# Stores of X held back by the kernel's own clocks, a last norm summed on TensorE, and conditioning blocks used with a margin

## The chip, the cores and the metric

One core of one Trainium2 chip runs the whole program; the seven other cores are idle. The time is device microseconds of one execution. Three runs of the kernel before gave 2848.49, 2847.53 and 2843.91 us, so their median is 2847.53 us. One more execution was recorded by the hardware profiler: 2844.86 us, of which 2843.1 us lie between its first and its last instruction (the span). Every duration below is from that execution.

## The reference

Two layers of a diffusion trunk are computed in float32 for 1152 positions of 1024 features each: 128 positions of a prompt, conditioned by `c_ctx`, and 1024 of a sample, conditioned by `c`.

```
for l in range(2):
    shift1, scale1, gate1, shift2, scale2, gate2 = split(silu(cond) @ w_ada[l] + b_ada[l])   # 1024 x 6144
    h = rmsnorm(x, norm_g[l, 0]) * (1 + scale1) + shift1
    y = attention_and_retention(h) @ w_o        # layer 0
    y = chunk_gmlp(h) @ w_out                   # layer 1
    x = x + gate1 * y
    h = rmsnorm(x, norm_g[l, 1]) * (1 + scale2) + shift2
    x = x + gate2 * ((silu(h @ w_gate) * (h @ w_up)) @ w_down)
y = x * rsqrt(mean(x * x, features) + 1e-6) * final_norm_g
```

The change touches the last line (the final norm), the way in which X is laid off in device memory, and the products with `w_ada` (the conditioning).

## The kernel before, in words

**Layout.** X stands transposed: 8 blocks of 128 features on the partitions, positions along the columns. The positions are cut into two chunks `c` of two pieces `h` with 288 columns each, so a piece of a feature block `f` is a tile of 128x288 (`xp(f, c, h)`), and `xp2` is two blocks side by side. Chunk 0 lies in the tiles x0 and x1, chunk 1 in x2 and x3. A factor of a product is split into a high and a low part (a cast on ACT, a subtraction on DVE or POOL), and each product of TensorE is three: high by high, high by low, low by high. Such a set of 24 products of 288 columns makes one feature block of one piece.

**Weights.** The class `Stream` loads all weights in one fixed order through three staging slots `ST` of 512 KB (issued by SP) and casts them into five ring slots `w`. `pump` takes the next item of the list as soon as a condition on the clocks holds, and in the order of the list alone. An item of kind `w` is a weight unit: its cast stands on ACT, its subtraction on DVE, and then its slot of `ST` is free. An item of kind `pair` is two blocks of `w_ada`: they are multiplied out of `ST` at once, by four products of 32x512 into one PSUM bank (`PS<-ST,S` in the rows), and then two of the three slots are free. Eight pairs make one third of a layer's conditioning.

**What sets the order.** Nothing runs by itself: the Python program writes each engine's instructions down in one order, and each engine works through its own queue in that order. To choose the order the program keeps rough clocks (`Clocks`): `clk.t["T"]` is where it believes TensorE to be, and `clk.ready(tiles)` when it believes that these tiles are written. `tick()` after each group of products calls `pump` and `fill`; `fill` writes down pieces of background work (norms, splits of activations) when the clocks say that their inputs are there. A pair is written down once `clk.ready` of its two blocks is not later than TensorE's clock. A store of X to device memory (`pspill` for two feature blocks of a piece) is written onto SP's queue at once, when its instruction that makes X has been written down; SP waits for that instruction and holds all loads behind it.

**Projection into X** (`proj_out`, once in each layer). 32 sets of 24 products are added to X (`resid`, DVE), squared (ACT) and summed (DVE). When a piece of chunk 0 is complete, `rscale` normalizes it in place (8 DVE and 8 ACT instructions for each piece), and `rsplit` makes seven split operands of it: casts of 128x576 on ACT, differences and subtractions of the same width on DVE. Meanwhile TensorE goes on with chunk 1 and needs a new weight unit for each set of 24 products there.

**The end of the program** (`mixer.run(last1, done1)`). The last group of the second FFN's output product is done for chunk 0 (`down`), then for chunk 1 by `down2`, first for the feature blocks 0, 1, 4, 5 and then for 2, 3, 6, 7. After each step `last1` puts the squares of the finished blocks into the background queue: Square on ACT into one of two buffers, an add on DVE into the running sum `acc2`, and on ACT the multiplication by the gain `final_norm_g`. When all eight blocks of a piece are in the sum, `rstd` sums over the partitions by six products with `ones` of two columns, takes the root (ACT) and the reciprocal (DVE) of 96x12 values, spreads them to a diagonal (DVE), and multiplies that by `ones` to get a 128x288 tile of factors for each piece (copied by ACT). `done1` then multiplies X by the factors, two blocks at a time (128x576, DVE), and stores each on SP's queue to the output.

Of the kernel before, what the change touches and what calls it, by code (L numbers as in the profile page):

```python
# [13 lines left out]
P = 128  # L14
# [118 lines left out]
def body(nc, tc, ap):  # L133
# [88 lines left out]
    class Stream:  # L222
# [11 lines left out]
        def pump(self, force=False):  # L234
            moved = True
            while moved:
                moved = False
                while self.di < min(self.hold, len(self.items)) and self.st:
                    it = self.items[self.di]
                    it["st"] = self.st.popleft()  # L240
                    n = 1
                    for d in it["shape"]:
                        n *= d
                    dst = ST[:, it["st"], :n]
                    if len(it["shape"]) == 2:
                        dst = dst.rearrange("p (a b) -> p a b", a=it["shape"][0])
                    it["v"] = dst
                    it["n"] = n
                    if it["load"] is not None:
                        it["load"](dst)  # L250
                    else:
                        SY.dma_start(out=dst, in_=it["src"])
                    self.di += 1
                    moved = True
                if self.pi < self.di and self.pi not in self.stops:
                    it = self.items[self.pi]
                    now = clk.t["T"] + 1.0
                    if it["kind"] == "block":
                        continue
                    if it["kind"] == "pair":  # L260
                        if self.pi + 1 >= self.di:
                            continue
                        two = self.items[self.pi + 1]
                        if not force and clk.ready([it["v"], two["v"]]) > clk.t["T"]:
                            continue
                        it["fn"](it["v"], two["v"])
                        self.st += [it["st"], two["st"]]
                        self.pi += 1
                    elif it["kind"] == "w":
                        if not self.ring:  # L270
                            continue
                        if not force and clk.ready([it["v"]]) > now:
                            continue
                        r = self.ring.popleft()
                        ring_new(r)
                        g = self.prep(it, r)
                        if att[0] and not force:
                            self.gens[r] = bg_add(g)
                        else:
                            run(g)  # L280
                        self.ready.append(r)
                    else:
                        if len(self.ring) < it["need"]:
                            continue
                        if not force and clk.ready([it["v"]]) > clk.t["T"]:
                            continue
                        it["fn"](it["v"])
                        self.st.append(it["st"])
                    self.pi += 1
                    moved = True  # L290
                    if force and it["kind"] == "w":
                        return
# [84 lines left out]
                moved = True  # L377

    def tick():
        W.pump()  # L380
        fill()

# [95 lines left out]
    def xp2(i, c, h):  # L478
        return xh(c, i // 2)[:, 2 * (i % 2):2 * (i % 2) + 2, h]

    def pspill(i, c, h):
        o = piece(c, h)
        SY.dma_start(out=xtd[:, 2 * i:2 * i + 2, o:o + HN], in_=xp2(i, c, h))

    def preload(c, q, h):
        o = piece(c, h)
# [73 lines left out]

    def xnorm(l, w, c):

        yield from rstd(c)
        A, B = acol[l][w], mod[l][:, 24 * w:24 * w + 8]
        ts = [SC[:, 1728 + HN * i:2016 + HN * i] for i in range(4)]
        for h in range(2):
            r = acc2(c)[:, HN * h:HN * h + HN]
            sg = psegs(c, h)
            dst = [[z[:, f, piece(c, h):piece(c, h) + HN] for f in range(8)] for z in (Hh, Hl)]

            def first(f):
                for cond, s in sg:
                    V.scalar_tensor_tensor(ts[f % 4][:, s], xp(f, c, h)[:, s], A[:, f, cond:cond + 1], r[:, s],
                                           ALU.mult, ALU.mult)

            def split(f):
                t, hi, lo = ts[f % 4], dst[0][f], dst[1][f]
                for cond, s in sg:
                    S.activation(R(hi[:, s]), t[:, s], AF.Identity, bias=B[:, f, cond:cond + 1])
                for cond, s in sg:  # L580
                    V.scalar_tensor_tensor(R(lo[:, s]), t[:, s], B[:, f, cond:cond + 1], hi[:, s], ALU.add, ALU.subtract)
            for f in range(3):
                first(f)
            for f in range(8):
                split(f)
                if f + 3 < 8:
                    first(f + 3)
                if f == 7:
                    hn[0] = 2 * c + h + 1
                yield  # L590
# [24 lines left out]

    def rscale(l, c, h):

        yield from rstd(c, (h,))
        A, B = acol[l][1], mod[l][:, 24:32]
        r = acc2(c)[:, HN * h:HN * h + HN]  # L620
        for f in range(10):
            if f < 8:
                for cond, s in psegs(c, h):
                    x = xp(f, c, h)[:, s]
                    V.scalar_tensor_tensor(x, x, A[:, f, cond:cond + 1], r[:, s], ALU.mult, ALU.mult)
            if f > 1:
                for cond, s in psegs(c, h):
                    x = xp(f - 2, c, h)[:, s]
                    S.activation(x, x, AF.Identity, bias=B[:, f - 2, cond:cond + 1])
            yield  # L630
        scaled.add((c, h))
# [1838 lines left out]
    yield "E"  # L2470


    def last1(c, m):
        for f in (m, m + 4):
            for h in range(2):
                x = xp(f, c, h)
                bg3.append(squares(c, h, f, lambda x=x, f=f: S.activation(x, x, AF.Copy, scale=P2[:, 19 + f:20 + f])))

    def done1(c):
        def gen():  # L2480
            yield from rstd(c)
            for h in range(2):
                r = acc2(c)[:, HN * h:HN * h + HN].unsqueeze(1).to_broadcast([P, 2, HN])
                for i in range(4):
                    x = xp2(i, c, h)
                    V.tensor_tensor(x, x, r, ALU.mult)
                    o = piece(c, h)
                    SY.dma_start(out=ap["o_y"][2 * i:2 * i + 2, :, o:o + HN].rearrange("f p t -> p f t"), in_=x)
                    yield
        g = bg_add(gen())  # L2490
        if c:
            drain(g)

    mixer.run(last1, done1)
    while bg:
# [56 lines left out]
```

## Time and profile before

| what | value |
|---|---|
| runs | 2843.91, 2847.53, 2848.49 us |
| median | 2847.53 us |
| profiled execution | 2844.86 us, span 2843.1 us |
| PE (TensorE) busy | 2689.3 us, 95% of the span |
| DVE, ACT, POOL busy | 63%, 41%, 18% |
| DMA | 457.67 MB, mean 161 GB/s |
| mean granted TensorE clock | 0.983 of full speed |

PE is busy nearly throughout, so time is to be looked for in the stretches in which it stands, and at the two ends. A row of the timeline gives the start, the time to the end of the last of its instructions, the engine, the operation with its output and inputs, their count, and in brackets how long the engine had stood and what it had waited for. All instructions are recorded by one helper and so carry one line number (L129); they are told apart by their tiles. `w` is the ring of weights, `hq` and `h` are split activations, `PS` is PSUM, `SC` scratch.

### The profile page before, as it was taken

Reading aid. Unit: us, or ns where it says so; the run is one execution under the profiler, and the core shown is the slowest. Engines: PE = TensorE matmul, PEld = TensorE weight load, DVE = VectorE, ACT = ScalarE, POOL = GpSimd, SP = SyncE. Lnnn points to the kernel's source line nnn. Section 1 sums busy time; section 2 is a strip of 40 time slices with the busy share of each in tenths; the row PEclk is TensorE's granted clock in tenths of the full one; section 3 lists DMA queues with packets and bytes.
Section 4 is the critical chain, followed back from the end, with each engine's and each line's share of the span. In section 5 each row is a group of like instructions: output and inputs, shape, how many; then the busy total and the mean of one; then the engine's idle time right before and its main releaser. Section 6 shows DMA issues by size and latency. Waiting matters only on the chain.

```text
span 2843.1 us, 49004 instructions
## 1 busy us (share of the span) xinstructions
PE 2689.3 (95%) x18859; PEld 2536.9 (89%) x18859; DVE 1787.7 (63%) x3606; ACT 1167.8 (41%) x2389; POOL 514.5 (18%) x570
## 2 busy tenths in 40 slices
PE   6989998999999999999999899998999999999996
PEld 5987897988988999999899877798999999999995
DVE  5651235888577565665788763456666666558876
ACT  5552224777455333333322351234544344332224
POOL 1120013665100000000465300000000000016551
PEclk9999998999999999999999999999999999999998
DMA  9386426323433444538877442352334343578761
GB/s 301 90 271 207 131 72 188 90 57 96 156 111 120 144 169 140 181 128 273 270 236 251 142 154 82 111 169 77 113 124 162 108 157 124 189 267 267 233 211 67
DMA packets 455328, 457.67 MB, mean 161 GB/s; under 512 B 25963, under 2 KB 399478, under 8 KB 453558
## 3 DMA queue, kind: packets, MB, share of 16 engines
q1 hardware_dynamic: 400272, 360.83, 41.3%
q10 hardware_dynamic: 54822, 93.70, 8.9%
q8 instruction: 149, 2.44, 0.4%
q14 instruction: 85, 0.70, 0.1%
HBM read 312.52 MB, written 141.93 MB: 160 GB/s over the span
## 4 chain that ended last, share of the span: by engine, by line
PE 62%; DVE 9%; ACT 4%; DMA 4%; issue 2%; POOL 1%; ACTq 0%; SPq 0%; DVEq 0%; POOLq 0%
PE PS L129 62%; DVE x L129 4%; DVE SC L129 2%; DVE w L129 2%; DMA hcd<-SC 2%; ACT x L129 1%; ACT w L129 1%; ACT SC L129 1%; DVE hq L129 1%; POOL ST L129 1%; DMA x<-xtd 0%; DMA w<-krd 0%; DMA ST<-in_w_ada 0%; DVE ST L129 0%; ACTq L129 0%
## 5 line engine op out<-in xcount | busy, mean ns | idle before, releaser
L129 PE MATMUL PS<-hq,w 128*128 128x288 f32 (+1 forms) x10644 | 1547.5, 302 | 62.6 <-ACT SC L129 16.2
L129 PEld LDWEIGHTS PS<-hq,w 128*128 128x128 f32 x10644 | 1484.3, 189 | 99.1 <-ACT w L129 20.8
L129 DVE TENSOR_TENSOR w<-ST,w 128x512 fp32r<-128x512 f32 (+3 forms) x539 | 382.1, 725 | 294.8 <-ACT w L129 290.4
L129 ACT CAST w<-ST 128x512 fp32r<-128x512 f32 (+3 forms) x717 | 375.2, 552 | 420.8 <-POOL ST L129 274.3
L129 DVE SCALAR_TENSOR_TENSOR x<-PS,mod,x 128x288 f32<-128x288 f32 (+2 forms) x944 | 389.5, 445 | 124.5 <-PE PS L129 119.4
L129 POOL TENSOR_TENSOR w<-ST,w 128x256 fp32r<-128x256 f32 (+1 forms) x178 | 126.9, 729 | 1592.2 <-ACT w L129 970.2
L129 PE MATMUL PS<-h,w 128*128 128x288 f32 (+1 forms) x2522 | 386.8, 298 | 10.7 <-DVE SC L129 7.3
L129 PEld LDWEIGHTS PS<-h,w 128*128 128x128 f32 (+1 forms) x2522 | 350.6, 188 | 21.5 <-DVE SC L129 9.7
L129 ACT COPY SC<-PS 128x576 f32<-128x576 f32 (+8 forms) x245 | 124.3, 510 | 259.8 <-PE PS L129 218.5
L129 PE MATMUL PS<-x,w 128*128 128x288 f32 (+1 forms) x1440 | 218.8, 299 | 1.8 <-ACT adac L129 1.4
L129 PEld LDWEIGHTS PS<-x,w 128*128 128x128 f32 x1440 | 203.0, 188 | 4.2 <-ACT h L129 1.8
L129 DVE TENSOR_TENSOR SC<-PS,SC 128x576 f32<-128x576 f32 (+3 forms) x146 | 94.1, 646 | 169.0 <-PE PS L129 149.0
L129 POOL TENSOR_TENSOR ST<-ST 128x256 f32<-128x256 f32 (+1 forms) x192 | 139.9, 729 | 150.6 <-DVE w L129 134.6
L129 PEld LDWEIGHTS PS<-w,hq 128*128 128x128 f32 x648 | 120.5, 188 | 38.9 <-issue 11.4
L129 PE MATMUL PS<-w,hq 128*128 128x512 f32 x648 | 154.6, 396 | 0.0
L129 DVE TENSOR_TENSOR SC<-SC 128x288 f32<-128x288 f32 (+5 forms) x215 | 104.4, 494 | 57.5 <-ACT SC L129 41.4
L129 ACT ACTIVATE SC<-SC 128x576 f32<-128x576 f32 (+2 forms) x89 | 56.9, 639 | 192.2 <-DVE SC L129 180.5
L129 PE MATMUL PS<-w,w 96*128 96x512 f32 x384 | 109.2, 420 | 4.7 <-ACT w L129 2.7
L129 DVE TENSOR_TENSOR SC<-SC,x 128x576 fp32r<-128x576 f32 (+1 forms) x90 | 68.0, 756 | 69.6 <-DMA hcd<-SC 50.7
L129 DVE TENSOR_REDUCE sm<-PS 128x1 f32<-128x1152 f32 (+1 forms) x72 | 89.0, 1236 | 21.9 <-PE PS L129 21.1
L129 ACT ACTIVATE SC<-x 128x288 f32<-128x288 f32 x128 | 55.2, 440 | 114.8 <-DVE x L129 92.4
L129 DVE TENSOR_TENSOR ST<-ST 128x512 f32<-128x512 f32 x144 | 98.8, 686 | 1.8
(191 smaller groups left out, 2475.9 us busy)
## 6 DMA issues: line engine op xcount, KB each, us to landing
hq<-hcd SPq DMA_DIRECT2D x106, 576.0 KB, 9.1
hcd<-x ACTq DMA_DIRECT2D x180, 288.0 KB, 2.2
ST<-in_w_ada SPq DMA_DIRECT2D x80, 512.0 KB, 4.2
h<-hcd SPq DMA_DIRECT2D x48, 576.0 KB, 7.3
ST<-in_w_ffn_gate SPq DMA_DIRECT2D x52, 512.0 KB, 4.0
ST<-in_w_ffn_up SPq DMA_DIRECT2D x52, 512.0 KB, 3.9
hcd<-SC ACTq DMA_DIRECT2D x72, 288.0 KB, 3.3
ST<-in_w_ffn_down SPq DMA_DIRECT2D x80, 256.0 KB, 5.4
```

Of the source, the lines that this page charges most:

```text
L129: return fn(*args, **kw)
```

## The change

1. In `pump`, a pair of conditioning blocks is written down only when TensorE's clock is 1.5 us past the time at which the blocks are believed to have landed (before: 0).
2. `pspill` puts a store of X into a list `due`; `spill_due`, called at each `tick`, writes it onto SP's queue once TensorE's clock is 3.0 us past the time at which X is believed to be made. `xnorm` and `rscale` first write down all stores of their piece that are still in the list.
3. At the end, chunk 0's second piece is scaled and stored after all products instead of between them. For chunk 1 the first four feature blocks go through the old running sum; the squares of the last four go each into a buffer of its own and are summed over features and partitions at once on PE, by float32 products of 128x288 with the 128x128 `ones` into two PSUM banks (ten products: eight squares and the two running sums). The root is taken on 128x288 values (ACT), the reciprocal too (DVE), and there are no diagonal, spreading products and copies any more. The multiplications by the gain stand in two groups of four after the squares, and chunk 1's eight stores alternate between ACT's and SP's queues.

```diff
@@ -261,7 +261,7 @@
                         if self.pi + 1 >= self.di:
                             continue
                         two = self.items[self.pi + 1]
-                        if not force and clk.ready([it["v"], two["v"]]) > clk.t["T"]:
+                        if not force and clk.ready([it["v"], two["v"]]) + 1.5 > clk.t["T"]:
                             continue
                         it["fn"](it["v"], two["v"])
                         self.st += [it["st"], two["st"]]
@@ -377,6 +377,7 @@
                 moved = True
 
     def tick():
+        spill_due()
         W.pump()
         fill()
 
@@ -478,9 +479,19 @@
     def xp2(i, c, h):
         return xh(c, i // 2)[:, 2 * (i % 2):2 * (i % 2) + 2, h]
 
+
+    due = deque()
+
     def pspill(i, c, h):
         o = piece(c, h)
-        SY.dma_start(out=xtd[:, 2 * i:2 * i + 2, o:o + HN], in_=xp2(i, c, h))
+        due.append((c, h, xtd[:, 2 * i:2 * i + 2, o:o + HN], xp2(i, c, h)))
+
+    def spill_due(which=None):
+
+        for z in list(due):
+            if z[:2] == which or which is None and clk.ready([z[3]]) + 3.0 < clk.t["T"]:
+                SY.dma_start(out=z[2], in_=z[3])
+                due.remove(z)
 
     def preload(c, q, h):
         o = piece(c, h)
@@ -560,6 +571,8 @@
 
     def xnorm(l, w, c):
 
+        for h in range(2):
+            spill_due((c, h))
         yield from rstd(c)
         A, B = acol[l][w], mod[l][:, 24 * w:24 * w + 8]
         ts = [SC[:, 1728 + HN * i:2016 + HN * i] for i in range(4)]
@@ -615,6 +628,7 @@
 
     def rscale(l, c, h):
 
+        spill_due((c, h))
         yield from rstd(c, (h,))
         A, B = acol[l][1], mod[l][:, 24:32]
         r = acc2(c)[:, HN * h:HN * h + HN]
@@ -2470,26 +2484,65 @@
     yield "E"
 
 
+    def gcol(c, h, f):
+        x = xp(f, c, h)
+        S.activation(x, x, AF.Copy, scale=P2[:, 19 + f:20 + f])
+
     def last1(c, m):
+        if c and m > 1:
+            return
         for f in (m, m + 4):
             for h in range(2):
-                x = xp(f, c, h)
-                bg3.append(squares(c, h, f, lambda x=x, f=f: S.activation(x, x, AF.Copy, scale=P2[:, 19 + f:20 + f])))
+                bg3.append(squares(c, h, f, lambda h=h, f=f: gcol(c, h, f)))
+
+    def scaled_out(c, h, r):
+        for i in range(4):
+            x = xp2(i, c, h)
+            V.tensor_tensor(x, x, r.unsqueeze(1).to_broadcast([P, 2, HN]), ALU.mult)
+            o = piece(c, h)
+            (SY if i % 2 or not c else S).dma_start(out=ap["o_y"][2 * i:2 * i + 2, :, o:o + HN].rearrange("f p t -> p f t"), in_=x)
+            yield
 
     def done1(c):
         def gen():
-            yield from rstd(c)
+            yield from rstd(0)
             for h in range(2):
-                r = acc2(c)[:, HN * h:HN * h + HN].unsqueeze(1).to_broadcast([P, 2, HN])
-                for i in range(4):
-                    x = xp2(i, c, h)
-                    V.tensor_tensor(x, x, r, ALU.mult)
-                    o = piece(c, h)
-                    SY.dma_start(out=ap["o_y"][2 * i:2 * i + 2, :, o:o + HN].rearrange("f p t -> p f t"), in_=x)
-                    yield
-        g = bg_add(gen())
-        if c:
-            drain(g)
+                if h:
+                    yield lambda: False
+                yield from scaled_out(0, h, acc2(0)[:, HN * h:HN * h + HN])
+        if c == 0:
+            bg_add(gen())
+            return
+        while bg3:
+            bg_step(bg3)
+
+
+        a = acc2(1)
+        sums = [PS[:, 4 + h, :HN] for h in range(2)]
+        root = [SC[:, 576 + HN * h:][:, :HN] for h in range(2)]
+        late = [(0, 2), (0, 3), (1, 6), (1, 7), (1, 2), (1, 3), (0, 6), (0, 7)]
+
+        def add(h, q, st, sp):
+            TE.matmul(sums[h], lhsT=ones, rhs=q, start=st, stop=sp, skip_group_check=True)
+        for n, (h, f) in enumerate(late):
+            q = SC[:, 1728 + HN * n:][:, :HN] if n < 6 else adac[:, 0:HN] if n == 6 else ST[:, 0, 0:HN]
+            S.activation(q, xp(f, 1, h), AF.Square)
+            add(h, q, n in (0, 2), n in (5, 7))
+            if n == 3:
+                for z in range(2):
+                    add(z, a[:, HN * z:HN * z + HN], False, False)
+        for f in (2, 3, 6, 7):
+            gcol(1, 1, f)
+        for h in (1, 0):
+            S.activation(root[h], sums[h], AF.Sqrt, bias=epsc, scale=1.0 / 1024.0)
+        for f in (2, 3, 6, 7):
+            gcol(1, 0, f)
+        while bg:
+            bg_step()
+        for h in (1, 0):
+            V.reciprocal(root[h], root[h])
+            for _ in scaled_out(1, h, root[h]):
+                pass
 
     mixer.run(last1, done1)
     while bg:
```

**Order on PE, where the second head group's keys are projected, just ahead of the retention's values (layer 0).** `ST,S` are the conditioning products of a pair, `hq,w` three chunks' products with one weight unit, `w,hq` the values' products; of the twelve equal rows `hq,w` ahead of it, the last five stand. Before:

```order
L129 MATMUL PS<-hq_20_535,w_32_1715 128x384 x6
L129 MATMUL PS<-ST,S_92 32x512 x4
L129 MATMUL PS<-hq_13_219,w_32_1715 128x384 x6
L129 MATMUL PS<-hq_17_331,w_32_1715 128x384 x6
L129 MATMUL PS<-hq_19_465,w_32_1715 128x384 x6
L129 MATMUL PS<-hq_20_535,w_32_1715 128x384 x6
L129 MATMUL PS<-ST,S_92 32x512 x4
L129 MATMUL PS<-w_33_1848,hq_13_219 128x512 x6
L129 MATMUL PS<-w_34_1852,hq_17_331 128x512 x6
L129 MATMUL PS<-w_35_1856,hq_19_465 128x512 x6
L129 MATMUL PS<-ST,S_92 32x512 x4
```

The same place now:

```order
L129 MATMUL PS<-hq_13_219,w_32_1715 128x384 x6
L129 MATMUL PS<-hq_17_331,w_32_1715 128x384 x6
L129 MATMUL PS<-hq_19_465,w_32_1715 128x384 x6
L129 MATMUL PS<-hq_20_535,w_32_1715 128x384 x6
L129 MATMUL PS<-ST,S_92 32x512 x4
L129 MATMUL PS<-w_33_1848,hq_13_219 128x512 x6
L129 MATMUL PS<-w_34_1852,hq_17_331 128x512 x6
L129 MATMUL PS<-w_35_1856,hq_19_465 128x512 x6
L129 MATMUL PS<-w_37_1970,hq_20_535 128x512 x6
L129 MATMUL PS<-ST,S_92 32x512 x4
```

The first pair shown has moved behind the four rows `hq,w` (24 products of 384 columns), and from there on four rows of the values' products stand between two pairs instead of three.

**Order on ACT in layer 1's `proj_out`, while chunk 0's second piece is normalized (`x<-x,mod`) and split (`hq<-x`, `h<-x`).** `w_141` to `w_143` are the weight units that PE needs next, one after the other; `SC<-x` are squares. Before:

```order
L129 CAST w_141_17535<-ST 128x1024
L129 ACTIVATE SC<-x_104_11716 128x288
L129 ACTIVATE x_101_11572<-x_101_11572,mod_94 128x288 x4
L129 ACTIVATE x_102_11573<-x_102_11573,mod_94 128x288 x4
L129 CAST hq_13_219<-x_101_11572 128x2x288 x2
L129 CAST hq_17_331<-x_102_11573 128x2x288 x2
L129 CAST h_139_17473<-x_102_11573 128x576 x2
L129 CAST hq_20_535<-x_101_11572 128x2x288 x2
L129 CAST hq_19_465<-x_102_11573 128x2x288 x2
L129 CAST h_138_17472<-x_101_11572 128x576 x2
L129 CAST h_140_17474<-x_102_11573 128x576 x2
L129 CAST w_142_17618<-ST 128x1024
```

The same place now:

```order
L129 CAST hq_13_219<-x_101_11572 128x2x288 x2
L129 CAST hq_17_331<-x_102_11573 128x2x288 x2
L129 CAST w_141_17560<-ST 128x1024
L129 ACTIVATE SC<-x_104_11716 128x288
L129 CAST h_139_17472<-x_102_11573 128x576 x2
L129 CAST hq_20_535<-x_101_11572 128x2x288 x2
L129 CAST w_142_17604<-ST 128x1024
L129 ACTIVATE SC<-x_104_11716 128x288
L129 CAST hq_19_465<-x_102_11573 128x2x288 x2
L129 CAST h_138_17471<-x_101_11572 128x576 x2
L129 CAST h_140_17473<-x_102_11573 128x576 x2
L129 CAST w_143_17649<-ST 128x1024
```

The unit w_141 has moved from ahead of the normalization to behind the first four casts of the split, and w_142 from behind the split into its middle.

**Order on DVE at the end of the program, after the last additions into X.** `x_156`, `x_157` are chunk 0, `x_158`, `x_159` chunk 1; `x<-x,SC` multiplies by the factors. One piece of the difference:

```order
-L129 TENSOR_TENSOR SC<-SC 128x288 x13
-L129 RECIPROCAL rs_100<-rs_100 96x12
-L129 TENSOR_TENSOR SC<-ident,rs_100 96x576
+L129 TENSOR_TENSOR x_156_22498<-x_156_22498,SC 128x2x288 x2
+L129 TENSOR_TENSOR x_157_22499<-x_157_22499,SC 128x2x288 x2
+L129 RECIPROCAL SC<-SC 128x288
 L129 TENSOR_TENSOR x_158_22500<-x_158_22500,SC 128x2x288 x2
 L129 TENSOR_TENSOR x_159_22642<-x_159_22642,SC 128x2x288 x2
+L129 RECIPROCAL SC<-SC 128x288
 L129 TENSOR_TENSOR x_158_22500<-x_158_22500,SC 128x2x288 x2
 L129 TENSOR_TENSOR x_159_22642<-x_159_22642,SC 128x2x288 x2
```

Thirteen adds of the running sums have gone from behind the last addition into X; chunk 0's four multiplications and two reciprocals over 288 columns have come.

## Rows read from the trace of the kernel before

**Rows 1.** The page: span and instructions, busy time of each engine.

```profile
span 2843.1 us, 49004 instructions
PE 2689.3 (95%) x18859; PEld 2536.9 (89%) x18859; DVE 1787.7 (63%) x3606; ACT 1167.8 (41%) x2389; POOL 514.5 (18%) x570
```

**Rows 2.** Waits: engine, for whom, us in total, times, longest.

```profile
PE PS L129 <- DMA ST<-in_w_ada: 7.6, 4, 2.9
PEld PS L129 <- DMA ST<-in_w_ada: 10.4, 8, 3.1
SPq L129 <- DVE x L129: 280.5, 59, 48.9
```

**Rows 3.** Timeline of PE, 229 to 258 us.

```profile
229.77 8.60 PE L129 MATMUL PS<-hq,w 128*128 128x384 f32 x48
241.25 2.87 PE L129 MATMUL PS<-ST,S 128*32 128x512 f32 x8 [2.88 <-DMA ST<-in_w_ada]
244.04 5.37 PE L129 MATMUL PS<-hq,w 128*128 128x384 f32 x24
249.34 1.06 PE L129 MATMUL PS<-ST,S 128*32 128x512 f32 x8
...
254.67 1.05 PE L129 MATMUL PS<-ST,S 128*32 128x512 f32 x4
256.85 1.05 PE L129 MATMUL PS<-ST,S 128*32 128x512 f32 x4 [1.13 <-DMA ST<-in_w_ada]
```

**Rows 4.** Windows: us, PE busy (count), granted clock, DMA share, GB/s.

```profile
244.00:246.00 2.00, 2.00 (x8) 0.50 0.75 225
1985.00:1990.00 5.00, 0.67 (x2) 0.50 0.00 0
2830.00:2834.00 4.00, 2.47 (x6) 0.50 0.01 2
```

**Rows 5.** Timeline of layer 1's proj_out, 1973 to 2001 us.

```profile
1973.32 2.39 ACT L129 CAST hq<-x 128x576 fp32r<-128x576 f32 x4
...
1988.23 1.04 ACT L129 CAST w<-ST 128x1024 fp32r<-128x1024 f32 x1
...
1989.33 0.85 PE L129 MATMUL PS<-hq,w 128*128 128x288 f32 x2 [9.47 <-ACT w L129]
...
1990.73 10.04 PE L129 MATMUL PS<-hq,w 128*128 128x288 f32 x64 [0.56 <-DVE w L129]
```

**Rows 6.** Timeline of PE in layer 0's proj_out, same stage.

```profile
803.49 5.65 PE L129 MATMUL PS<-hq,w 128*128 128x288 f32 x22 [4.08 <-DVE w L129]
...
810.81 8.69 PE L129 MATMUL PS<-hq,w 128*128 128x288 f32 x64 [0.73 <-DVE w L129]
```

**Rows 7.** Timeline of the end of the program, 2816 to 2843 us.

```profile
2816.88 0.96 PE L129 MATMUL PS<-h,hq 128*128 128x288 f32 x6
...
2817.68 0.93 DVE L129 SCALAR_TENSOR_TENSOR x<-PS,mod,x 128x288 f32<-128x288 f32 x2
...
2828.10 2.08 PE L129 MATMUL PS<-ones,SC 128*96 128x2 f32 x12 [10.26 <-DVE SC L129]
...
2833.02 0.40 ACT L129 COPY SC<-PS 128x288 f32<-128x288 f32 x1 [2.54 <-PE PS L129]
2833.45 5.44 DVE L129 TENSOR_TENSOR x<-x,SC 128x576 f32<-128x576 f32 x8 [1.85 <-ACT SC L129]
2833.98 0.40 ACT L129 COPY SC<-PS 128x288 f32<-128x288 f32 x1 [0.56 <-PE PS L129]
```

**Rows 8.** Groups of instructions: busy us, mean ns; squares of the end from 2790.

```profile
L129 ACT ACTIVATE SC<-x 128x288 f32<-128x288 f32 x19 | 8.2, 432 | 13.4 <-DVE SC L129 10.8 <-DVE x L129 2.6
L129 DVE RECIPROCAL sm<-sm 128x1 f32<-128x1 f32 x72 | 10.5, 156 | 11.4 <-ACT SC L129 11.3
L129 DVE RECIPROCAL rcn<-rcn 128x18 f32<-128x18 f32 x4 | 1.1, 266 | 9.0 <-ACT rcn L129 9.0
```

**Rows 9.** The output's stores: us from issue to landing.

```profile
DMA to landing us min/median/max: 2.2/2.3/3.0
```

## The prediction

> **What bounds the kernel now.** I read the page's busy times first: PE works 2689.3 us of the 2843.1 us span, 95% [rows 1]. No other engine comes near, so an edit pays only where it shortens a stretch in which PE stands or runs slowly, or the tail behind PE's last product. Second the waits, for who stands for whom: PE stood 7.6 us in four places for blocks of w_ada, and SP's queue 280.5 us for the instructions that make X [rows 2]. Third the timeline around those places, and the windows for the clock: where PE had just stood, the granted clock was 0.50, the lower level of 1.2 GHz [rows 4], so a stall costs more than its gap. Fourth the timeline of the last 27 us.
>
> The terms are summed against the profiled execution, 2844.86 us (1.76 outside its span). It lies 2.67 below the median of the runs, 2847.53, and inside their spread; I carry the difference over to the median.
>
> **Part 1, the margin: -7.2 us.** The first stalled pair stands behind 48 products that end at 229.77+8.60 = 238.37; the next pair starts at 249.34 [rows 3]. These 10.97 us held one pair (1.06) and 24 products, worth half of 8.60 = 4.30 but taking 5.37 after the stall, at clock 0.50. So 10.97-1.06-4.30 = 5.6 us were lost. Now the 24 products stand ahead of that pair, which PE reaches at 242.67. The blocks had landed by 244.04-1.06 = 242.98 at the latest, as the second four products ran to 244.04. That leaves at most 0.3 us: gain 5.3 to 5.6, I take 5.4. Two pairs on, a pair begun at 254.67 ended only at 257.90: 3.23-1.06 = 2.17 lost, since its second block came late. One more group of the values' products ahead of it adds (254.67-250.40)/3 = 1.42 us, so 1.4 to 2.17: I take 1.8. The other 7.6-2.88-1.13 = 3.6 us of the waits lie in layer 1, at pairs that stand where they stood among PE's products: nothing. Part 1 lies between 0 (the loads slip with the pairs) and -7.8; what a slipping load could cost beyond that is the last rival.
>
> **Part 2, the stores: -3.5 us.** The 280.5 us on SP's queue are no time of PE's. The stores' own move I put at nothing: SP takes a load up sooner, but the load still needs a free staging slot, which the casts give. What counts is what the earlier loads do to the written order in layer 1's proj_out. There PE stood from 1989.33-9.47 = 1979.86 for the cast of a weight unit, which ACT did at 1988.23, behind four casts of the split that began at 1973.32 and more of the same piece; PE ran through from 1990.73 [rows 5]. The 10.87 us held two products worth 0.136 each (8.69/64, [rows 6]), so 10.6 were lost, and the 64 products that follow took 10.04 instead of 8.69: together 11.95.
>
> Now the units w_141 and w_142 stand among the split's casts. Layer 0's proj_out has such an order already and its stall stays: from 803.49-4.08 = 799.41 to 810.81 less 24x0.136 = 3.3 us of products is 8.1 us lost [rows 6]. The difference is 3.8. DVE still makes the split's subtractions and each unit's own, so I take -3.5, between 0 (DVE was the limit all along) and -12 (nothing of the stall is left). No wait is added: before a piece is normalized its stores are written down, so they still read X ahead of its change.
>
> **Part 3, the final norm: -7.1 us.** PE's last ordinary product ends at 2816.88+0.96 = 2817.84, DVE's last addition at 2817.68+0.93 = 2818.61. The eight last multiplications end at 2833.45+5.44 = 2838.89 [rows 7], and the span 4.2 later, with stores that land 2.2 to 3.0 us after their issue [rows 9]. This last stretch I keep. Between lay the running sum's adds, a wait of PE of 10.26 us, and products and copies at clock 0.50.
>
> After: four squares and sums may be done earlier; PE adds the rest behind 2817.84. The two old spreading products were 0.96 apart by ACT's copies (2833.02, 2833.98) [rows 7], at clock 0.50 [rows 4]; at full clock that is 0.48. The first piece's sum is closed by the eighth product: 2817.84+8x0.48 = 2821.7. ACT's last two squares (0.43 each, [rows 8]) follow DVE's addition at 2818.61 and end near 2819.5, ahead of that, as do the four gain multiplications. Root 0.40 and its handing over: 2822.3. No row has a reciprocal of 288 columns. One column takes 156 ns and 18 take 266 [rows 8]: 6.47 ns per column, so 0.156+287x0.00647 = 2.01 us. Four multiplications take 4x0.68 = 2.72. Both pieces one after the other on DVE: 2822.3+2x(2.01+2.72) = 2831.76, or 2838.89-2831.76 = 7.1 earlier. Chunk 0's four moved multiplications, 2.72 us, fit on DVE between 2818.61 and 2821.7, while it waits for the root; without that cover they cost 2.72.
>
> Bounds: a reciprocal as fast as a multiplication of 576 columns (0.68) gives -9.8; one that scales with the 18-column row (266/18x288 = 4.26) gives -2.6. If PE has fallen to clock 0.50 by 2817.84, the eight products last to 2825.5: -3.3. Both ill bounds together: +1.2. I stay with 2.01 us, since two rows give a slope, and with full clock, since PE has just been busy.
>
> The Trainium skill ("VectorE: DVE Perf Modes", section "First, the fixed hardware budget") says that a reciprocal is an iterative divide with a repeat count of 8. If the repeats were eight cycles per column at that page's 0.96 GHz, 288 columns would be an estimated 2.55 us with the 156 ns row as a start, and part 3 would give -6.0. The slope of the rows, 6.47 ns, is below its 8.3; no row here shows 288 columns.
>
> **Sum.** -7.2-3.5-7.1 = -17.8. 2844.86-17.8 = 2827.1 for the profiled execution; 2847.53-17.8 = 2829.7 for the median.
>
> **The rivals.**
>
> Only the final norm counts: the gains in the middle are given back where PE next waits for weights, because DMA and casts set the pace there. For it: the 4.30 us of products that fill the first stall consume weights earlier. Against it: no staging load other than w_ada's is named beside PE's waits [rows 2]. 2847.53-7.1 = 2840.4.
>
> The stall of proj_out goes altogether, since ACT's casts alone made it, as the wait for ACT ahead of 1989.33 says [rows 5]. Against it: layer 0 waits for DVE there [rows 6]. -7.2-12-7.1 = -26.3: 2821.2.
>
> The tail is weak: PE cold while it adds up, so part 3 gives -3.3. The clock was 0.50 in the old tail [rows 4], but behind a wait of 10.26 us. -14.0: 2833.5.
>
> Slower: a pair holds two of the three staging slots until its products, so a later pair delays the weight loads behind it, and PE waits for those units instead. About 13 pairs of layer 0 move. At the price of the late block above, 2.17 us each, they cost 28.2, and with -17.8 the kernel is 10.4 slower: 2857.9. It decides from the ninth pair on (9x2.17 = 19.5). Against it: a pair that had to wait frees its slots no later now (the first by 242.98+1.06 = 244.04, as before), and most moves are a group or two of 1.42 us.
>
> **How the numbers follow.** The forecast, -10 to -23, has 0.64; the final norm alone 0.13; the stall gone 0.10; a weak tail 0.06; slower 0.07. A change below 0.2%, 5.7 us, can't be told from none in a measurement of this kernel. Faster: 0.64+0.10+0.06, and 0.07 of the final norm alone, whose 7.1 is near the bound, = 0.87. Same: its other 0.06 and 0.02 of the slower case = 0.08. Slower: 0.05. The range 2819 to 2841 holds the forecast but for 0.02, the weak tail, most of the vanished stall (0.08) and half of the final norm alone: 0.82. The likeliest case's own range is 2824.5 to 2837.5.
>
> **What would show it.** Part 1: behind the products that end at 238.4, PE goes on with 24 products at full clock, and no wait for w_ada of 2.9 us is left near 241; the waits for w_ada fall from 7.6 to about 3.6. Part 2: in layer 1's proj_out PE's longest wait is below 9.47, with DVE and not ACT as its releaser; an unchanged 9 us puts this term at zero. Part 3: about eight products of 128x288 with ones follow PE's last ordinary one within 4 us, the reciprocals last about 2.0 us each, and the last multiplication ends some 14 us after PE's last ordinary product, not 21. Wrong would be: new waits of PE for weight units between 250 and 450 us, or a tail in which the reciprocals or the roots come later than 2826 would be here.

## The result

The changed kernel takes 2830.13 us (median of 6 runs) against 2848.01 us of the kernel before (6 runs); the ratio is 0.9947, with a 95% interval of 0.9933 to 0.9960, or 15.1 us less (11.4 to 19.1). The forecast was 2829.7 us. The total was right, but not each of its three terms: one hit to a tenth of a microsecond, one was near, and one was priced at about twice what the traces show for it, because I had read an event of one execution as a rule.

The page of the changed kernel, as in [rows 1]:

```profile
span 2836.4 us, 48993 instructions
PE 2700.4 (95%) x18863; PEld 2551.8 (90%) x18863; DVE 1790.7 (63%) x3598; ACT 1167.9 (41%) x2388; POOL 515.0 (18%) x570
```

This execution (2838.38 us) was the slowest of the six, and its span is only 6.7 us below that of [rows 1]. The waits, as in [rows 2]:

```profile
PE PS L129 <- ACT w L129: 14.3, 9, 3.4
PE PS L129 <- DVE w L129: 12.3, 9, 4.1
...
PE PS L129 <- DMA ST<-in_w_ada: 3.6, 4, 2.7
...
SPq L129 <- DVE x L129: 154.6, 35, 50.3
```

PE's wait for blocks of w_ada in `ST` has gone from 7.6 to the 3.6 us that were forecast, and no wait for w is longer than 4.1 us. SP's wait for X is down by 126 us, which is, as argued, no time of PE's.

**Near 241 us.** The timeline of PE, against [rows 3]:

```profile
237.16 1.06 PE L129 MATMUL PS<-ST,S 128*32 128x512 f32 x8
238.15 12.76 PE L129 MATMUL PS<-hq,w 128*128 128x384 f32 x72
250.84 1.06 PE L129 MATMUL PS<-ST,S 128*32 128x512 f32 x8
251.83 5.78 PE L129 MATMUL PS<-w,hq 128*128 128x512 f32 x24
257.54 2.06 PE L129 MATMUL PS<-ST,S 128*32 128x512 f32 x8
```

72 products instead of 48 stand ahead of the pair at 250.84, and 24 instead of 18 products of the values ahead of the next. No pair has to be waited for at its start, and the granted clock is 1.00 (the window 231 to 251 us below). The second block of the pair at 257.54 still comes late: its eight products take 2.06 us instead of 1.06. So of the 5.6 and 2.17 us lost before, 1.0 is left.

**Layer 1's proj_out**, against [rows 5], and then four windows: the start, the pairs above, this stage and the tail (us, busy time and instructions of PE, of its weight loads PEld, of DVE, ACT and POOL, granted clock, DMA share, GB/s):

```profile
1970.22 15.74 PE L129 MATMUL PS<-hq,w 128*128 128x288 f32 x116
1988.86 4.70 PE L129 MATMUL PS<-hq,w 128*128 128x288 f32 x22 [2.90 <-DVE w L129]
1994.92 0.53 PE L129 MATMUL PS<-hq,w 128*128 128x288 f32 x2 [1.35 <-ACT w L129]
1996.34 8.36 PE L129 MATMUL PS<-hq,w 128*128 128x288 f32 x40 [0.89 <-DVE w L129]
```

```profile
22.00:42.00 20.00, 15.34 (x124) 13.14 (x125) 9.88 (x29) 10.34 (x24) 0.00 (x0) 0.74 1.02 322
231.00:251.00 20.00, 20.00 (x120) 18.66 (x122) 3.21 (x4) 5.26 (x11) 0.00 (x0) 1.00 0.56 178
1986.00:2000.00 14.00, 8.90 (x39) 8.44 (x40) 13.35 (x22) 7.33 (x12) 0.00 (x0) 0.73 0.29 83
2818.00:2826.00 8.00, 5.71 (x27) 4.31 (x25) 6.36 (x9) 5.72 (x13) 0.00 (x0) 1.00 0.43 150
```

One wait of 9.47 us for ACT has become three of 2.90, 1.35 and 0.89 us, the first for DVE, which works 13.35 of 14 us.

**The tail**, against [rows 7]:

```profile
2817.90 0.96 PE L129 MATMUL PS<-h,hq 128*128 128x288 f32 x6
...
2818.70 4.04 PE L129 MATMUL PS<-SC,ones 128*128 128x288 f32 x16
...
2822.78 0.50 ACT L129 ACTIVATE SC<-PS,epsc 128x288 f32<-128x288 f32 x1 [1.18 <-PE PS L129]
...
2823.32 1.95 DVE L129 RECIPROCAL SC<-SC 128x288 f32<-128x288 f32 x1 [1.22 <-ACT SC L129]
...
2825.30 2.77 DVE L129 TENSOR_TENSOR x<-x,SC 128x576 f32<-128x576 f32 x4
...
2827.99 1.95 DVE L129 RECIPROCAL SC<-SC 128x288 f32<-128x288 f32 x1
2829.97 2.77 DVE L129 TENSOR_TENSOR x<-x,SC 128x576 f32<-128x576 f32 x4
```

From PE's last ordinary product (2818.86) to the last multiplication (2832.74) it is 13.9 us; in the kernel before it was 21.05. All the steps of the forecast stand there one behind the other: products at full clock, a root, and twice a reciprocal and four multiplications on DVE.

**Why the span shows only 6.7 us.** Both programs hold the same instructions in the same order on every engine until past 200 us; still the changed kernel's trace is 6.7 us late by then. Its sample rows were waited for longer at the start, and the clock then fell to half (0.74 on average from 22 to 42 us, in the window above):

```profile
23.28 4.26 PE L129 MATMUL PS<-ident,h 128*128 128x128 f32 x24 [2.51 <-DMA h<-in_x_sample]
29.92 4.54 PE L129 MATMUL PS<-hq,w 128*128 128x384 f32 x12 [2.38 <-ACT hq L129]
```

In the kernel before the same stretch ran at full clock:

```profile
22.00:42.00 20.00, 14.10 (x139) 11.29 (x139) 12.36 (x38) 13.92 (x37) 0.00 (x0) 1.00 1.02 321
```

So two single traces can't be subtracted from end to end. The experiments below are read stage by stage instead, over all 14 traces.

### The profile page after: what moved, and what is told of

Same layout as the page of the kernel before. It is cut to its first block, busy times and chain, and to the rows that moved or that the text cites. A ratio compares the mean times of both kernels' runs of the same rounds, so it can differ in the third digit from the quotient of the medians.

```text
span 2836.4 us, 48993 instructions
## 1 busy us (share of the span) xinstructions
PE 2700.4 (95%) x18863; PEld 2551.8 (90%) x18863; DVE 1790.7 (63%) x3598; ACT 1167.9 (41%) x2388; POOL 515.0 (18%) x570
## 4 chain that ended last, share of the span: by engine, by line
PE 70%; DVE 10%; DMA 4%; ACT 4%; issue 3%; POOL 1%; ACTq 0%; SPq 0%; DVEq 0%; POOLq 0%
PE PS L129 70%; DVE x L129 4%; DVE w L129 2%; DVE SC L129 2%; DMA hcd<-SC 2%; ACT x L129 1%; ACT w L129 1%; ACT SC L129 1%; DMA ST<-in_w_in_c 1%; DVE hq L129 1%; POOL ST L129 1%; DMA rgd<-SC 0%; DMA w<-krd 0%; DVE ST L129 0%; ACTq L129 0%
## 5 line engine op out<-in xcount | busy, mean ns | idle before, releaser
L129 POOL TENSOR_TENSOR ST<-ST 128x256 f32<-128x256 f32 (+1 forms) x192 | 140.7, 733 | 150.6 <-DVE w L129 134.6
L129 PEld LDWEIGHTS PS<-w,hq 128*128 128x128 f32 x648 | 120.1, 188 | 40.2 <-issue 11.4
```

The costliest lines, as they stand in the source:

```text
L129: return fn(*args, **kw)
```

## The experiments

**The three parts apart, and the whole again.** The edits are the numbered parts of the change, each put alone into the kernel before (with `spill_due` in the second, and all of `last1` and `done1` in the third):

```diff
-                        if not force and clk.ready([it["v"], two["v"]]) > clk.t["T"]:
+                        if not force and clk.ready([it["v"], two["v"]]) + 1.5 > clk.t["T"]:
```

> The kernel before with the margin of 1.5 us alone (part 1). Theory (the three parts add up, each by its own mechanism): 7.2 us faster (5 to 8), the 2.9 us wait for a block of w_ada near 241 us is gone and PE runs its 24 products ahead of the pair at full clock; the 9.5 us stall in layer 1's proj_out is still there. Rival (the pairs' gain is given back at later waits, or came in truth from the stores' order): within 2 us of no change.

```diff
-        SY.dma_start(out=xtd[:, 2 * i:2 * i + 2, o:o + HN], in_=xp2(i, c, h))
+        due.append((c, h, xtd[:, 2 * i:2 * i + 2, o:o + HN], xp2(i, c, h)))
```

> The kernel before with the delayed stores alone (part 2). Theory: 3.5 us faster (0 to 12), PE's stall of 9.5 us in layer 1's proj_out falls to 4 to 7 us and its releaser becomes DVE; the pairs near 241 us still stall. Rival (DVE was the limit of that stage all along): 0, with a stall of the same 10 us in all.

```diff
     def last1(c, m):
+        if c and m > 1:
+            return
...
+            add(h, q, n in (0, 2), n in (5, 7))
```

> The kernel before with the new end of the program alone (part 3). Theory: 7.1 us faster (6.5 to 7.5), nearly all from the tail: 13.9 us from PE's last ordinary product to the last multiplication, against 21.05 before. Rival (one of the other two parts carried the whole result and the tail gives 3 us or less).

The fourth is the changed kernel itself.

> The changed kernel once more, for a second trace. Its profiled execution so far lost 5 us to the kernel before within the first 45 us, where both programs are the same instructions in the same order. Theory (that is chance in the landing of the first rows and in the clock of the start): this trace starts about as the one of before does and its span is near 2827 us. Rival (the change itself makes the start later): the 5 us are there again. The total of the three parts, 17.8 us, should show in the ratio: 0.9937.

Measured, as ratio to the kernel before with its interval, and in us of 2848. The runs of this section stand in three sets, each on another chip and each with its own runs of the kernel before, to which its ratios refer:

| kernel | ratio | interval | us |
|---|---|---|---|
| e1_margin | 0.9982 | 0.9967 to 0.9996 | -5.1 |
| e2_stores | 0.9994 | 0.9981 to 1.0007 | -1.7 |
| e3_norm | 0.9977 | 0.9962 to 0.9992 | -6.6 |
| e4_again | 0.9944 | 0.9926 to 0.9961 | -16.0 |

The three alone add up to -13.4, the whole is -16.0 and was -15.1: within these intervals (about 4 us to each side) they add, and no part carries the result alone. For the size of one part the times are too coarse; the traces are finer. e4_again has a span of 2829.4 us, and its first 200 us took 182.0 us against 187.5 in the first trace of the same kernel: the late start did not come again.

The unexpected thing is in the traces of e2 and e3, which have the old order near 241 us. This is PE in e3:

```profile
231.29 8.60 PE L129 MATMUL PS<-hq,w 128*128 128x384 f32 x48
239.81 1.06 PE L129 MATMUL PS<-ST,S 128*32 128x512 f32 x8
...
252.70 1.05 PE L129 MATMUL PS<-ST,S 128*32 128x512 f32 x4 [1.12 <-DMA ST<-in_w_ada]
```

The same 48 products, the same pair behind them, and no wait; only the late second block (1.12 us) is there again. The reason can be followed back on ACT, first in the kernel before, then in e3:

```profile
228.41 0.59 ACT L129 CAST SC<-PS 128x512 fp32r<-128x512 f32 x1 [11.21 <-DMA knd<-SC]
```

```profile
225.07 0.59 ACT L129 CAST SC<-PS 128x512 fp32r<-128x512 f32 x1 [7.96 <-DMA knd<-SC]
```

ACT waits there for a store of keys to land before it may write its buffer again; behind this cast stand the weight unit's cast and, on SP behind the values' stores, the loads of w_ada. SP issued those 3.3 us later in the kernel before than in e3; the two rows are in that order:

```profile
237.12 21.16 SPq L129 DMA_DIRECT2D ST<-in_w_ada  x9
233.79 25.66 SPq L129 DMA_DIRECT2D ST<-in_w_ada  x10
```

In the profiled execution of the kernel before the wait was 11.2 us, in the five other traces of the old order 8.0 to 8.4 us (in e9 4.5 of it were filled with copies). The 2.88 us wait of [rows 3] was seen in that one trace out of six; in e12 PE started this pair without a wait, but its second block came late, and the eight products took 2.09 us instead of 1.06.

**The stages over all traces.** Each stage is the time between the same two instructions on DVE (subtractions of a weight's low part, an addition into X, at 478 us a reduction), named by their times in the kernel before. Worked out from the traces' start times, in us:

```
stage             margin 0: before e2 e3 e8 e9 e12           margin 1.5: after e1 e4 e6 e7 e10           3.0: e11  6.0: e5
  20 to  201     180.8 185.6 179.9 181.6 183.1 181.2     187.5 183.3 182.0 183.2 180.8 184.5          182.5     183.2
 201 to  478     277.0 272.5 273.1 272.9 273.1 272.1     271.7 272.1 269.5 270.3 269.9 271.3          270.5     278.9
1600 to 1743     142.8 147.5 144.9 143.7 145.2 147.0     145.6 143.6 143.9 143.5 143.7 143.3          153.3     155.2
                 old order: before e1 e3 e9              late stores: after e2 e4 e5 e7 e8 e10 e11 e12
1959 to 2112     152.8 150.7 150.6 152.3                 147.6 147.4 146.2 149.5 146.3 147.8 149.6 149.7 146.5
```

From 201 to 478 us the margin is worth 273.45-270.79 = 2.7 us on average, 1.9 without the trace that had the late landing; from 1600 to 1743 us, where I had put it at nothing, 145.2-143.9 = 1.3, which is less than the spread of the traces there. In layer 1's proj_out the late stores are worth 151.6-147.8 = 3.8 us, and the two groups do not overlap (e6, whose edit changes this stage, is left out; it took 148.5). In the tail it is 13.86 or 13.87 us in all traces with the new end but e7's, and 20.97 to 21.33 in the five with the old one.

**Which stores matter (e8).** In the kernel before, with `spill_due`:

```diff
     def pspill(i, c, h):
         due.append((c, h, xtd[:, 2 * i:2 * i + 2, o:o + HN], xp2(i, c, h)))
+        if not held[0]:                 # True from layer 1's proj_out on
+            spill_due((c, h))
```

> The kernel before with the delayed stores in layer 1's proj_out alone; elsewhere each store is written down at once. Theory (all that the delayed stores gain is the order of the casts in this one stage): the stage is as in the changed kernel, with waits of PE for w of about 2.9, 1.4 and 0.9 us in place of 9.5 and 0.6, and every other stage as before. Rival (the other stores matter as well): part of the 9.5 us stays. Also one more trace of the old order near 241 us: if its 2.9 us wait is the rule there it is seen again, if it was chance it is not.

It took 2844.24 us. PE in the stage:

```profile
1986.73 4.44 PE L129 MATMUL PS<-hq,w 128*128 128x288 f32 x22 [2.95 <-DVE w L129]
1992.79 0.53 PE L129 MATMUL PS<-hq,w 128*128 128x288 f32 x2 [1.62 <-ACT w L129]
1994.20 5.56 PE L129 MATMUL PS<-hq,w 128*128 128x288 f32 x40 [0.88 <-DVE w L129]
```

The three short waits are all there with the stores delayed in this one stage; e1_margin, with the old stores, has the old wait:

```profile
1988.35 0.85 PE L129 MATMUL PS<-hq,w 128*128 128x288 f32 x2 [9.47 <-ACT w L129]
```

The stage takes 147.8 us in e8, as with all stores delayed. So the gain of part 2 comes from this stage's stores. That they gain by the written order, and not by loads that land sooner, can be read in the kernel before. The three slots are filled and cast in order, so the unit for which PE stood 9.47 us was loaded by the first of these two:

```profile
1934.93 3.56 SPq L129 DMA_DIRECT2D ST<-in_w_out_c  x2
```

Its cast came 53 us later, at 1988.23 [rows 5], with no wait of ACT in front of it: it had stood behind the casts of the split.

**The price of a late pair (e5, e11) and of none (e12).** In the changed kernel:

```diff
-                        if not force and clk.ready([it["v"], two["v"]]) + 1.5 > clk.t["T"]:
+                        if not force and clk.ready([it["v"], two["v"]]) + 6.0 > clk.t["T"]:    # e5; e11: 3.0; e12: nothing
```

> The changed kernel with the margin raised from 1.5 to 6.0 us, so that many more pairs move, and further. The rival of the prediction (a late pair holds two of three staging slots, so the weights behind it come late) expects a loss that grows with the margin: some 20 moved pairs at up to 2.17 us, 10 to 40 us slower than the changed kernel, with new waits of PE for weight units in the windows where pairs are. The theory (pairs late by a few us cost nothing, since the units behind them are cast well ahead of their use) expects within 4 us of the changed kernel, and waits for w_ada at or under its 3.6 us.

> The changed kernel with a margin of 3.0 us. At 6.0 the kernel lost some 22 us against 1.5. Theory (the loss comes from pairs held so long that the units behind them in the three staging slots are late, which begins somewhere above 1.5): between the two, 0 to 12 us slower than the changed kernel, with the loss in the stretches 200 to 478 and 1600 to 1743 us. Rival (the loss is a step reached only near 6): within 3 us.

> The changed kernel without its margin (delayed stores and the new end alone). Theory (the margin's part is the late second block, 2.1 us, and now and then a late landing worth 4 more): 2 to 4 us slower than the changed kernel, about 0.9955 of the kernel before; from 200 to 478 us 272.5 to 273.1 (or 277 with the late landing) against 269.5 to 272.1. Prediction's own price: 7.2 us slower, 0.997.

Measured: margin 6.0 gives 1.0019 (1.0006 to 1.0031), slower than the kernel before; 3.0 gives 0.9975 (0.9961 to 0.9990); none 0.9967 (0.9954 to 0.9981); 1.5, in the two measurements, 0.9947 and 0.9944. So the theory that late pairs cost nothing fell: against 1.5 a margin of 6.0 loses some 21 us, 3.0 some 8, and none some 6, though there the intervals overlap. The stage table has the places: with 3.0 the loss is from 1600 to 1743 us (153.3 against 143.9), with 6.0 also from 201 to 478 us. This is e5 at the worst wait, on PE, ACT and SP:

```profile
1691.59 1.06 PE L129 MATMUL PS<-ST,S 128*32 128x512 f32 x8
1698.73 0.80 PE L129 MATMUL PS<-w,hq 128*128 128x512 f32 x1 [6.07 <-ACT w L129]
...
1695.80 1.94 ACT L129 ACTIVATE hq<-SC,mod 128x160 fp32r<-128x160 f32 x6 [1.05 <-DVE SC L129]
1697.64 1.03 ACT L129 CAST w<-ST 128x1024 fp32r<-128x1024 f32 x1
...
1686.19 0.38 SPq L129 DMA_DIRECT2D ST<-in_w_in_c  x1
```

The weight unit's load was issued at 1686.19, ahead of the pair's products, but it stands after the pair in the list; its cast is therefore written down only once the pair is, and by then ACT's queue holds a normalization. The cast's row names no wait, so it waited only for its turn, and PE stood 6.07 us. In e11 the same wait is 4.64 us:

```profile
1690.64 0.79 PE L129 MATMUL PS<-w,hq 128*128 128x512 f32 x1 [4.64 <-ACT w L129]
```

The mechanism of the prediction's slower rival is real, then; what delays PE is the place of the cast on ACT's queue. By e12 the margin is worth 6.0 us in time (about 0.6 to 11.4, from the two intervals; I had expected 2 to 4), and by e1 5.1; the traces account for 2.7 and perhaps 1.3 of that. Whether there is more to it than that stays open within these intervals.

**A late landing made on purpose (e9, e10).** In both kernels, at the cast of the first value block behind the keys:

```diff
+                if t == 6:
+                    for _ in range(18):
+                        nc.scalar.copy(junk, ones[:, :32])
```

> The kernel before with 18 small copies of 32 columns put on ACT ahead of the cast that stood at 228.4 us in its trace (nothing reads them, and the written order is otherwise the same), about 3.3 us of ACT's time. In that trace ACT stood 11.2 us there for a store of keys to land, in three other traces of the same order 8 us. Theory (this late landing alone made the 2.9 us wait for w_ada near 241 us): the wait is back, 2 to 3.5 us, with half clock behind it. Rival (something else made it, as the landing of the conditioning block itself): no wait of over 1.2 us.

> The changed kernel with the same 18 copies at the same place. Theory (the margin's 24 products cover a landing that is late by 3.3 us): no wait for w_ada over 0.5 us, and from 200 to 478 us a time as in the changed kernel's other traces, about 270 to 272 us against 277 in the kernel before with such a wait. Rival (the margin moves the wait behind the 24 products): 2 us or more.

This one failed by its design. In e9:

```profile
220.03 4.47 ACT L1273 COPY junk<-ones 128x32 f32<-128x32 f32 x18
228.39 0.59 ACT L129 CAST SC<-PS 128x512 fp32r<-128x512 f32 x1 [3.89 <-DMA knd<-SC]
```

The copies took 4.47 us and wait for nothing, so they ran while ACT would have stood for the landing anyway, and delayed nothing: no wait near 241 us in either kernel but the second block's (0.8 us) in e9. That the landing made the wait is read from the traces, and not shown by an experiment.

**What is left of proj_out's stall (e6).** In the changed kernel:

```diff
-                    V.tensor_tensor(R(lo), src[op][g], hi, ALU.subtract)
+                    (G if g and op in (2, 3, 4, 6) else V).tensor_tensor(R(lo), src[op][g], hi, ALU.subtract)
```

> The changed kernel with four of the seven low parts of a split (operands 2, 3, 4 and 6), in their second half, subtracted by POOL and not by DVE: 4x0.7 = 2.8 us less on DVE for each piece. Theory (DVE is what is left of the stall in layer 1's proj_out, where it works without a gap): PE's waits there for DVE's and ACT's part of w, 5.1 us in the changed kernel's trace, fall by 1.5 to 3. Rival (the written order on ACT, or POOL's own time of about 1.6 us for each, sets the end): the waits stay, or grow.

Measured 0.9939 (0.9924 to 0.9955), not to be told from the changed kernel. PE's waits in the stage did not fall (5.01 and 0.99, in all 6.0 us, against 5.1); PE and then DVE:

```profile
1989.10 0.85 PE L129 MATMUL PS<-hq,w 128*128 128x288 f32 x2 [5.01 <-ACT w L129]
1990.94 11.48 PE L129 MATMUL PS<-hq,w 128*128 128x288 f32 x64 [0.99 <-DVE w L129]
...
1989.08 1.80 DVE L129 TENSOR_TENSOR w<-ST,w 128x1024 fp32r<-128x1024 f32 x1 [1.57 <-ACT w L129]
```

The theory's fall did not come, but the run does not decide between theory and rival, for two reasons. First, DVE was hardly relieved. Where a subtraction of DVE starts while one of POOL's is running, it ends late; the one of 128x1024 above takes 1.80 us instead of the 1.22 of its equals, and ends 1.08 us after POOL's ended at 1989.80. Three instructions of DVE in this stage (1.98 instead of 0.75, 1.80 and 1.60 instead of 1.22 us) so give back 2.2 of the 2.7 us that the four moved ones save. Second, the edit also changed the written order on ACT: the cast of w_142, at 1983.03 in the changed kernel, stands behind four more casts of the split, at 1988.00. The long wait for ACT that comes back with this order fits the reading of part 2; which engine sets what is left of the stall stays open.

**Part of the tail on POOL (e7).** In the changed kernel's `scaled_out`:

```diff
-            V.tensor_tensor(x, x, r.unsqueeze(1).to_broadcast([P, 2, HN]), ALU.mult)
+            (G if c and i in ((1, 3) if h else (2,)) else V).tensor_tensor(x, x, r..., ALU.mult)
```

> The changed kernel with three of the eight last multiplications on POOL (two of the first piece, one of the second). Theory (after the sums the tail is DVE's time alone: two reciprocals of 1.95 and eight multiplications of 0.69 us): DVE's chain falls from 9.4 to 7.4 us and the span's end with it, 1.5 to 2.1 us earlier. Rival (POOL, at an estimated 1.6 us a multiplication from its 0.73 us for 256 columns, or the two engines' reads of one memory, takes it back): the last multiplication, now POOL's, ends no earlier.

Measured 0.9943 (0.9928 to 0.9958): no gain. The tail, from the first multiplication on:

```profile
2816.98 2.63 DVE L129 TENSOR_TENSOR x<-x,SC 128x576 f32<-128x576 f32 x2
2817.03 3.84 POOL L129 TENSOR_TENSOR x<-x,SC 128x576 f32<-128x576 f32 x2 [40.48 <-DVE SC L129]
...
2819.53 1.94 DVE L129 RECIPROCAL SC<-SC 128x288 f32<-128x288 f32 x1
2821.51 3.30 DVE L129 TENSOR_TENSOR x<-x,SC 128x576 f32<-128x576 f32 x3
```

A row with more than one instruction hides what happens here. The second of DVE's first two multiplications, by itself:

```profile
2817.66 1.95 DVE L129 TENSOR_TENSOR x<-x,SC 128x576 f32<-128x576 f32 x1
```

It starts while POOL's first (2817.03 to 2818.99) is running and ends 0.62 us after that one, which is about what a multiplication takes alone (0.69). DVE's first took 0.76. So the two engines took turns, a whole instruction each, and DVE's multiplications for the two pieces took 2.63 and 3.30 us where four on DVE alone take 2.77. The last one ends 14.3 us after PE's last product, 0.4 later than in the changed kernel. The reciprocal that ran beside POOL's second multiplication kept its 1.94 us. The rival holds; no version that beats the changed kernel was found.

## Why the prediction was right, and where it was not

**Part 3 (-7.1): right, step by step.** The tail fell from 21.05 to 13.87 us, by 7.2 us; a tail of 13.9 us was forecast. The slope of the two reciprocal rows gave 2.01 us and the trace has 1.95; the clock stayed full (1.00 from 2818 to 2826 us); the eight products up to the first piece's sum took 0.5 us each. e3_norm alone: -6.6. My estimate of 2.55 us for a reciprocal, worked out from the Trainium skill ("VectorE: DVE Perf Modes", section "First, the fixed hardware budget") with its repeat count of 8 read as eight cycles per column, does not hold: the measurement decides, and it sides with the slope of the rows.

**Part 2 (-3.5): right in place and size.** The stage is 3.8 us shorter on average over 13 traces, PE's longest wait there fell from 9.47 to 2.90 us, and its releaser is now DVE. That the stage of layer 0, with such an order, could stand for layer 1's after the change was a good measure. What I could not see is that the trace of the kernel before was itself on the long side: 152.8 us against 150.6 or 150.7 in e1 and e3, and 152.3 in e9; against that one trace the gain is 5.0 us, so the closeness of 3.5 to 3.8 is in part luck. e2_stores' time alone (-1.7, interval -5.4 to +2.0) neither confirms nor refutes it.

**Part 1 (-7.2): right mechanism, wrong size.** The step that failed is "So 10.97-1.06-4.30 = 5.6 us were lost ... gain 5.3 to 5.6, I take 5.4". It was lost in that execution; in none of the five other traces of the same order did PE stand ahead of that pair. The second term, the block that comes late (2.17 us with both its halves, I took 1.8), recurs in every trace of the old order, with waits of 0.8 to 1.1 us and 2.0 us lost on average. With the margin of 1.5 that pair is no longer late, but the one ahead of it is, by 0 to 1.0 us (0.4 on average), so this term is worth 1.6. The traces give 2.7 us on average, in place of 7.2 for the stretch to 478 us, and perhaps 1.3 in layer 1, which I had put at nothing. The times are too coarse to settle it: e1 alone gives 5.1 us (1.1 to 9.4), and 7.2 and 2.7 both lie inside. The sum by traces is -2.7-1.3-3.8-7.2 = -15.0, beside -15.1 and -16.0 in time; the forecast's -17.8 lies inside the first interval, and its overshoot is this term. That the sum meets the time to 0.1 us is chance, with intervals of 4 us to each side.

**The rivals.** "Only the final norm counts" fell with e1 (interval 0.9967 to 0.9996) and the stage table. "The stall goes altogether" fell: 2.90, 1.35 and 0.89 us are left, and which engine sets them e6 does not tell. "The tail is weak" fell. "Late pairs delay the units behind them" is not what 1.5 us does (from 250 to 450 us, where the prediction looked for new waits of PE for weight units, there are none in the changed kernel), but it is what 3.0 and 6.0 us do; I had called the number of moved pairs what decides (the ninth); at 3.0 us nearly all of the loss lies in one stage, where one cast held back on ACT's queue costs PE 4.64 us.

## What to carry to other kernels

A stall read from one profiled execution is a rule only if its cause is the program's order; where its releaser is a transfer, look at a second trace of the same instructions before its whole length goes into a sum. Where a kernel's time varies by more than the gain looked for, compare stages between the same instructions over several traces instead of end times. A margin against late transfers is a size with two sides: here 3 and 6 us are worse than 1.5, and 0 probably is.

## What the runs showed of the hardware that was not expected

- In e6 and e7 multiplications and subtractions of DVE and POOL took turns, a whole instruction each: a DVE multiplication of 128x576 (0.69 us alone) that started beside one of POOL's took 1.95 us and ended 0.62 us after it (e7), and subtractions of 128x1024 (1.22 alone) took 1.80 and 1.60 and ended 1.08 us after POOL's (e6). The reciprocal of 128x288 (1.95 alone, 1.94 beside POOL's) was not slowed.
- The same stretch from 20 to 201 us, with the same instructions in the same order, took from 179.9 to 187.5 us over 14 traces, which is half of what the whole change gains.
- The same wait for a store of keys was 8.0 to 8.4 us in five traces of the old order and 11.2 in one, and a wait of 2.88 us of PE followed it there.
